# Gate and up sums of a SwiGLU feed-forward as Strassen block products on one Trainium2 core

## The chip, the cores and the metric

The program runs on one core of one Trainium2 chip. The metric is the device time of one execution in microseconds (us). A core has engines that run side by side, each with its own queue in a fixed order: TensorE (PE, matrix products; PEld is its weight load), VectorE (DVE), ScalarE (ACT), GpSimd (POOL) and SyncE (SP), which here issues most transfers. The transfers themselves run on 16 DMA engines. SBUF is the working memory of 128 partitions, PSUM the memory that takes the products.

## The reference

Two decoder layers over 512 tokens of 1024 features: layer 0 mixes with a causal Conformer convolution, layer 1 with differential attention. Each is followed by a SwiGLU feed-forward of 2816 hidden features and by a gated per-layer embedding. The change touches the first line of the feed-forward:

```python
def rms_norm(x, g):
    xf = x.astype(jnp.float32)
    y = xf * lax.rsqrt(jnp.mean(xf * xf, axis=-1, keepdims=True) + EPS)
    return (y * g.astype(jnp.float32)).astype(x.dtype)

def swiglu(x, w_gate, w_up, w_down):
    return (jax.nn.silu(x @ w_gate) * (x @ w_up)) @ w_down
...
    h = x
    for i in range(DEPTH):
        ...
        u = rms_norm(h, ffn_norm_g[i])
        h = h + swiglu(u, ffn_w_gate[i], ffn_w_up[i], ffn_w_down[i])
        gate = jax.nn.sigmoid(rms_norm(h, ple_norm_g[i]) @ ple_w_gate[i])
        h = h + gate * (p[i] @ ple_w_proj[i])
```

## The kernel before

Activations lie transposed: h[c] (L166) holds 128 features by 512 tokens, eight of them. Every product of two float32 matrices is made of three products of float32r parts: a value is split into a rounded part (hi) and the rest (lo), and mm3 (L153 to L157) adds lo x hi, hi x lo and hi x hi in PSUM. One mm3 over a block of 128 features is three matmuls, each with its own weight load.

A weight tile is 128 x 1024, 512 KB: 128 output features by 1024 inputs, in eight blocks of 128 (wpart, L159). weight() (L137) takes the next tile of the program's order: a transfer on SP's queue into wraw (two buffers), a cast on ACT into whi (L148), a subtraction on DVE, or for a few tiles on POOL, into wlo (L150). whi and wlo have four buffers each, so weights run up to four tiles ahead.

Norm (L172) holds the scaled activations norm.u as 8 pairs of hi and lo tiles (tags A0 to A15). The scale per token isn't applied there: squares are added on POOL (L189), columns() sums them with small products, POOL takes the power (L214), and rows() spreads the result over the partitions into rb, which is multiplied into the sums afterwards.

ffn() (L566) cuts the 22 hidden chunks of 128 into parts of 8, 8 and 6 (PARTS). For each chunk it takes a gate and an up tile, adds 8 blocks x 3 matmuls of 512 tokens for each into PSUM (tags mm with four banks, sc and tp with two each), multiplies both by rb (L582, L584, DVE), applies Silu (L583, ACT), multiplies (L585) and splits the result into hl (L587, L588, tag B). After a part linear() (L538) multiplies its hidden chunks by w_down, two outputs at a time for the first two, one at a time after, and adds them to h (L592). Then ple() (L598) makes the gated embedding; its factors pp wait since the stage before, those of chunks 6 and 7 of layer 0 in one of the two buffers of tag C4, those of layer 1 in one each of C2, C3 and C4 and in D2 and D3. The last chunk of layer 1's ple runs in two cuts of 256 tokens (CUTS, L52).

Tags name buffers: sb(shape, tag, bufs) gives one of bufs buffers and waits until one is free. The order of each engine's queue is not written out by hand; a list scheduler places the instructions by priority (the order of the program) and by its own times. wk (4 buffers) and big (5) are scratch tiles of 512 tokens.

Of the kernel before, what the change touches and what calls it, by code (L numbers as in the profile page):

```python
# [12 lines left out]
F32 = mybir.dt.float32  # L13
F32R = mybir.dt.float32r
# [6 lines left out]
P = 128  # L21
# [57 lines left out]
GLO = 1  # L79
QKV = (("q", 0, (0, 0, 0, 0)), ("v", 0, (0, 1, 1, 0)), ("q", 1, (1, 1, 2, 2)), ("q", 2, (0, 1, 2, 0)), ("v", 1, (1, 2, 2, 2)), ("q", 3, (0, 2, 0, 1)))  # L80
# [3 lines left out]
def trunk(ctx, tc, xT, pT, wts, diag, dww, vec, rel, onehot, lamv, out):  # L84
# [22 lines left out]
    f = lambda ap: ap.bitcast(F32)  # L107

# [240 lines left out]
    def phased_out(c):  # L349
# [5 lines left out]
        both_ = sb([P, 2, S], f"B{c}", 1)  # L355
# [12 lines left out]
    def other_taps(c):  # L368
# [13 lines left out]
        yc = sb([P, 2, S], f"B{c}", 1)  # L382
# [183 lines left out]
    def ffn(norm, after):  # L566
        rb = None
        for at, (f0, n) in enumerate(PARTS):
            hid = []
            for i in range(n):  # L570
                wg, wu = weight(), weight()
                pg, pu = mm(), mm()
                for k in range(NC):
                    mm3(pg, wpart(wg, k), norm.u[k], k == 0, k == NC - 1)
                if rb is None:
                    norm.diagonal()
                for k in range(NC):
                    mm3(pu, wpart(wu, k), norm.u[k], k == 0, k == NC - 1)
                if rb is None:
                    rb = norm.rows()  # L580
                tg, tu = big(), big()
                V.tensor_tensor(tg, pg, rb, ALU.mult)  # L582
                A.activation(tg, tg, AF.Silu)  # L583
                V.tensor_tensor(tu, pu, rb, ALU.mult)  # L584
                V.tensor_tensor(tu, tu, tg, ALU.mult)  # L585
                hl = sb([P, 2, S], f"B{i}", 1, F32R)
                A.copy(hl[:, 0], tu)  # L587
                V.tensor_tensor(hl[:, 1], tu, f(hl[:, 0]), ALU.subtract)  # L588
                hid.append((hl[:, 0], hl[:, 1]))

            def add(m, acc):
                V.tensor_tensor(h[m], acc, h[m], ALU.add)  # L592
                if at == len(PARTS) - 1:
                    after.chunk(m)

            linear(n, hid, add, 2)
# [30 lines left out]
    ffn(norm, n2)  # L627
# [65 lines left out]
    def values(s, ws, tb, between):  # L693
        acc, r = tokens(ws, tb, between)
        vt_ = sb([P, 4, 2, P], f"B{4 * s + tb}", 1, F32R)
# [217 lines left out]
    ffn(norm, n2)  # L913
# [132 lines left out]
```

## Time and profile before

| what | value |
|---|---|
| time, 3 runs | 1306.6, 1307.61, 1310.06 us (median 1307.61) |
| span of the profiled execution | 1308.0 us |
| 0 to 229 us, convolution | PE busy 216.8, DVE 166.1, POOL 101.1 us |
| 229 to 613 us, feed-forward and ple of layer 0 | PE 384.0 of 384, DVE 174.8, ACT 114.9, POOL 20.6 us |
| 613 to 905 us, attention | PE 279.2 of 292, DVE 218.4, POOL 111.8 us |
| 905 to 1274 us, feed-forward and ple of layer 1 | PE 369.0 of 369, DVE 163.1, ACT 108.1, POOL 14.6 us |

The profile is that of one execution, taken by the hardware profiler. A group or timeline row reads: line, engine, operation, output tile <- input tiles, output shape <- input shape, count, then the busy time and the mean duration of one in ns, then the idle time of the engine before it and what ended it. L numbers are lines of the kernel before. Consecutive instructions of one engine overlap at their ends, so what one costs its queue is read from the starts of a row of them. The windows view gives the busy time of each engine in a stretch of the span, the TensorE clock that was granted there (1.00 is full speed), the share of time that the 16 DMA engines were busy and the bytes moved per second.

### The profile page before, as it was taken

The numbers are of one execution on the slowest core, as the hardware profiler recorded it, in microseconds if no ns is written. First come the engines' busy times: TensorE is split into PE (matmuls) and PEld (weight loads), VectorE is DVE, ScalarE is ACT, GpSimd is POOL, SyncE is SP. The second block draws the span as 40 slices with busy tenths as digits, with TensorE's granted clock in tenths as the row PEclk, the third lists the DMA queues.
The fourth block names the chain that finished last, engine by engine and source line by source line (L and its number), as shares of the span: only waits on it lengthen the run. The fifth ranks groups of instructions, "written<-read, shape, count | busy, mean of one in ns | idle before, by whom it ended". The sixth has DMA issues, their size and how long they took to land. (4 is left out here: it accounts for less than half of the span.)

```text
span 1308.0 us, 15405 instructions
## 1 busy us (share of the span) xinstructions
PE 1278.6 (98%) x5904; PEld 1055.7 (81%) x5904; DVE 741.2 (57%) x1142; ACT 522.1 (40%) x827; POOL 248.2 (19%) x207
## 2 busy tenths in 40 slices
PE   8999999999999999999999998999999999999998
PEld 5888678888888888888888886878888888888887
DVE  6898646444344434456678888845543344334445
ACT  5642445332122212254566667734332233223332
POOL 4754323000000000032335535122000000000030
PEclk8999889999999999999999998999999999999999
DMA  6654313322323232232222211213323223222231
GB/s 219 229 166 156 106 33 129 96 98 87 106 96 97 88 104 94 80 122 83 80 91 92 89 58 59 87 48 114 97 97 97 97 97 97 97 97 89 83 119 65
DMA packets 46838, 131.97 MB, mean 101 GB/s; under 512 B 5379, under 2 KB 9987, under 8 KB 46764
## 3 DMA queue, kind: packets, MB, share of 16 engines
q1 hardware_dynamic: 44640, 127.55, 29.6%
q10 hardware_dynamic: 2124, 3.43, 0.8%
q8 instruction: 46, 0.75, 0.2%
q14 instruction: 28, 0.23, 0.1%
HBM read 126.75 MB, written 4.21 MB: 100 GB/s over the span
## 5 line engine op out<-in xcount | busy, mean ns | idle before, releaser
L148 ACT CAST whi<-wraw 128x1024 fp32r<-128x1024 f32 (+2 forms) x214 | 218.6, 1026 | 566.3 <-PE mm L157 349.5
L155 PE MATMUL mm<-A,wlo 128*128 128x512 f32 (+1 forms) x1096 | 423.9, 391 | 4.8 <-ACT A L169 2.7
L156 PE MATMUL mm<-A,whi 128*128 128x512 f32 (+1 forms) x1096 | 428.0, 392 | 0.4
L157 PE MATMUL mm<-A,whi 128*128 128x512 f32 (+1 forms) x1096 | 425.3, 389 | 0.0
L150 DVE TENSOR_TENSOR wlo<-wraw,whi 128x1024 fp32r<-128x1024 f32 (+2 forms) x210 | 260.5, 1244 | 70.9 <-ACT whi L148 70.6
L155 PEld LDWEIGHTS mm<-A,wlo 128*128 128x128 f32 x1096 | 206.2, 188 | 49.6 <-DVE wlo L150 3.7
L156 PEld LDWEIGHTS mm<-A,whi 128*128 128x128 f32 x1096 | 206.6, 188 | 46.4 <-DVE A L170 3.0
L157 PEld LDWEIGHTS mm<-A,whi 128*128 128x128 f32 x1096 | 206.6, 188 | 43.1 <-issue 1.0
L189 POOL TENSOR_TENSOR acc<-acc,wk 128x512 f32<-128x512 f32 x42 | 67.4, 1604 | 787.7 <-issue 660.2
L156 PE MATMUL mm<-B,whi 128*128 128x512 f32 x352 | 137.5, 391 | 0.0
L157 PE MATMUL mm<-B,whi 128*128 128x512 f32 x352 | 137.5, 391 | 0.0
L155 PE MATMUL mm<-B,wlo 128*128 128x512 f32 x352 | 137.2, 392 | 0.0
L592 DVE TENSOR_TENSOR h<-mm,h 128x512 f32<-128x512 f32 x48 | 33.0, 691 | 122.7 <-PE mm L157 122.7
L584 DVE TENSOR_TENSOR big<-mm,rb 128x512 f32<-128x512 f32 x44 | 30.4, 691 | 126.2 <-PE mm L157 126.2
L582 DVE TENSOR_TENSOR big<-mm,rb 128x512 f32<-128x512 f32 x44 | 30.4, 691 | 99.4 <-PE mm L157 93.0
L157 PEld LDWEIGHTS mm<-B,whi 128*128 128x128 f32 x352 | 66.1, 188 | 14.6
L155 PEld LDWEIGHTS mm<-B,wlo 128*128 128x128 f32 x352 | 66.1, 188 | 14.2
L156 PEld LDWEIGHTS mm<-B,whi 128*128 128x128 f32 x352 | 66.0, 188 | 14.2
L157 PE MATMUL mm<-whi,A 128*128 128x512 f32 x192 | 75.6, 395 | 0.0
L156 PE MATMUL mm<-wlo,A 128*128 128x512 f32 x192 | 75.0, 396 | 0.0
L155 PE MATMUL mm<-whi,A 128*128 128x512 f32 x192 | 74.8, 397 | 0.0
L214 POOL TENSOR_TENSOR r<-v,mhalf 128x8 f32<-128x8 f32 (+1 forms) x31 | 47.4, 1529 | 122.8 <-DVE v L212 100.4
(198 smaller groups left out, 1402.0 us busy)
## 6 DMA issues: line engine op xcount, KB each, us to landing
wraw<-in_wts SPq DMA_DIRECT2D x194, 512.0 KB, 3.5
wraw<-in_wts SPq DMA_DIRECT2D x16, 384.0 KB, 2.9
D<-in_diag SPq DMA_DIRECT2D x22, 256.0 KB, 4.9
C<-in_diag SPq DMA_DIRECT2D x16, 256.0 KB, 4.7
h<-in_xT SPq DMA_DIRECT2D x8, 256.0 KB, 5.6
bias<-scr ACTq DMA_DIRECT2D x8, 256.0 KB, 3.3
out_t<-h SPq DMA_DIRECT2D x7, 256.0 KB, 2.0
wraw<-in_wts SPq DMA_DIRECT2D x4, 256.0 KB, 5.2
```

Of the source, the lines that this page charges most:

```text
L148: A.copy(hi[:, cut], raw[:, cut])
L150: eng.tensor_tensor(lo[:, cut], raw[:, cut], f(hi[:, cut]), ALU.subtract)
L155: T.matmul(acc, al, bh, start=first, stop=False)
L156: T.matmul(acc, ah, bl, start=False, stop=False)
L157: return T.matmul(acc, ah, bh, start=False, stop=last)
L189: self.last = self.eng.tensor_tensor(self.acc, self.acc, sq, ALU.add)
L214: last_pow[0] = G.tensor_tensor(r[:, :n], v[:, :n], mhalf[:, :n], ALU.pow)
L582: V.tensor_tensor(tg, pg, rb, ALU.mult)
L584: V.tensor_tensor(tu, pu, rb, ALU.mult)
L592: V.tensor_tensor(h[m], acc, h[m], ALU.add)
```

## The change

The gate sum of two neighbouring chunks is a product of a 256 x 1024 weight block by 1024 x 512 activations. The change halves all three sides: the outputs (chunk c and chunk c+1), the inputs (blocks 0 to 3 and 4 to 7) and the tokens (0 to 255 and 256 to 511), and takes Strassen's seven products of half blocks in place of eight; the same for the up sum. It does so for 10 of the 11 pairs of chunks of each feed-forward. The first pair (PLAIN) keeps the old code.

- combinations(), once per feed-forward, scales h by the gain on ACT, makes the five sums and differences of activation blocks on POOL, each 128 x 1024, and splits each on ACT and DVE; the two other operands are halves of norm.u. They live in buffers of the tags in SPACE.
- operands() makes the weight sides of the seven products. Tile z takes the first half of one weight tile and the second half of the other, by SP; d, its difference, is made on POOL. Tile x is loaded by SP with the first halves of both tiles, and a transfer on POOL's queue adds the second halves to it in flight (accum_op). Tile y is loaded with the first weight tile, and a transfer adds the second. So there are three plain and two adding transfers of 512 KB where there were two plain ones. Each of z, x, y (128 x 1024) and d (128 x 512) is split on ACT and DVE.
- strassen() makes the products, each of 4 blocks x 3 matmuls of 256 tokens, and sums them to o1 and o2: one copy and two half copies on ACT, four operations on DVE.
- After the gate's two outputs, the gain rb is applied on DVE for one and on POOL for the other; the same for the up outputs; then product and split for both as before. Each of o1 and o2 holds half the tokens of one chunk and half of the other, which the strided writes of spot() sort out.
- B tiles are now allocated in pairs (btile), in the convolution and the attention too.

```diff
@@ -77,6 +77,13 @@
 PACK = True
 E1 = True
 GLO = 1
+H2 = S // 2
+SPACE = (
+    ((("C0", 2, 4), ("C1", 2, 4), ("C2", 2, 4), ("C3", 2, 4), ("wth", 2, 2), ("wtl", 2, 2)), ("C5", "C5"), "C4"),
+    ((("C0", 2, 4), ("C1", 2, 4), ("C5", 2, 4), ("D0", 1, 2), ("D1", 1, 2), ("D4", 1, 2), ("D5", 1, 2), ("wth", 2, 2), ("wtl", 2, 2)), ("C2", "C3"), "C4"),
+)
+PLAIN = ((0, 0),)
+DMASUM = True
 QKV = (("q", 0, (0, 0, 0, 0)), ("v", 0, (0, 1, 1, 0)), ("q", 1, (1, 1, 2, 2)), ("q", 2, (0, 1, 2, 0)), ("v", 1, (1, 2, 2, 2)), ("q", 3, (0, 2, 0, 1)))
...
@@ -105,6 +112,13 @@
     wk = lambda dt=F32, shape=(P, S): sb(list(shape), "wk", 4, dt)
     big = lambda dt=F32, shape=(P, S): sb(list(shape), "big", 5, dt)
     f = lambda ap: ap.bitcast(F32)
+    bpair = [None]
+    def btile(i, dt=F32):
+        if i % 2 == 0:
+            bpair[0] = sb([P, 2, 2, S], f"B{i // 2}", 1, dt)
+        return bpair[0][:, i % 2]
...
@@ -563,30 +577,167 @@
     linear(NC, z, add_conv, 3, first=(None, last_add[0], scaled[1]))
-    def ffn(norm, after):
+    def ffn(norm, after, space):
         rb = None
+        homes, xtags, ztag = space
+        slots = [(t, n, k) for t, n, k in homes for _ in range(n)]
+        def home():
+            t, n, k = slots.pop(0)
+            if k == 4:
+                w = sb([P, 4, H2], t, n, F32R)
+                return [w[:, 0:2], w[:, 2:4]]
+            two = [sb([P, 2, H2], t, n, F32R)]
+            t, n, k = slots.pop(0)
+            return two + [sb([P, 2, H2], t, n, F32R)]
+        def combinations():
+            us = [sb([P, 2, 2, S], f"B{1 + j}", 1) for j in range(2)]
+            us = [t.rearrange("p a b s -> p (a b) s") for t in us]
+            for c in range(NC):
+                A.activation(us[c // 4][:, c % 4], h[c], AF.Copy, scale=col(norm.g, c))
+            b = [[us[k][:, :, t * H2 : (t + 1) * H2] for t in range(2)] for k in range(2)]
+            sums = sb([P, 2, 2, S], "B3", 1).rearrange("p a b (u s) -> p a (b u) s", u=2)
+            made = {}
+            for i, (name, x, y, op) in enumerate((
+                (3, b[1][1], b[0][1], ALU.subtract), (4, b[0][0], b[1][0], ALU.subtract),
+                (1, b[0][0], b[1][1], ALU.add),
+                (6, b[0][0], b[0][1], ALU.add), (7, b[1][0], b[1][1], ALU.add),
+            )):
+                if not DMASUM and name in (3, 4):
+                    x, y = y, x
+                t = sums[:, i % 2]
+                G.tensor_tensor(t, x, y, op)
+                his, los = home(), home()
+                for k in range(2):
+                    A.copy(his[k], t[:, 2 * k : 2 * k + 2])
+                    V.tensor_tensor(los[k], t[:, 2 * k : 2 * k + 2], f(his[k]), ALU.subtract)
+                made[name] = [(his[k // 2][:, k % 2], los[k // 2][:, k % 2]) for k in range(4)]
+            made[2] = [tuple(t[:, :H2] for t in norm.u[k]) for k in range(4)]
+            made[5] = [tuple(t[:, H2:] for t in norm.u[4 + k]) for k in range(4)]
+            return made
+        def source(i, mstep, kh):
+            return bass.AP(wts.tensor, wts.offset + i * P * 1024 + kh * S, [[1024, P], [mstep, 2], [1, S]])
+        turn = [0]
+        def two_parts(raw, shape=(P, 1024)):
+            hi = sb([P, 1024], "whi", 4, F32R)
+            lo = sb([P, 1024], "wlo", 4, F32R)
+            n = raw.shape[-1]
+            A.copy(hi[:, :n], raw)
+            V.tensor_tensor(lo[:, :n], raw, f(hi[:, :n]), ALU.subtract)
+            return hi, lo
+        def operands(i):
+            m2 = 2 * P * 1024
+            turn[0] += 1
+            z = sb([P, 2, S], ztag, 2 if ztag[0] == "C" else 1)
+            nc.sync.dma_start(z, source(i, m2 + S, 0))
+            x = sb([P, 2, S], xtags[turn[0] % 2], 2)
+            nc.sync.dma_start(x, source(i, m2, 0))
+            y = sb([P, 1024], "wraw", 2)
+            nc.sync.dma_start(y, wts[i])
+            nc.gpsimd.dma_start(x, source(i, m2, 1), accum_op=ALU.add)
+            nc.gpsimd.dma_start(y, wts[i + 2], accum_op=ALU.add)
+            z = z.rearrange("p a s -> p (a s)")
+            d = big()
+            G.tensor_tensor(d, z[:, :S], z[:, S:], ALU.subtract)
+            zp = two_parts(z)
+            dp = two_parts(d)
+            xp = two_parts(x.rearrange("p a s -> p (a s)"))
+            yp = two_parts(y)
+            half = lambda w, j: tuple(t[:, j * S : (j + 1) * S] for t in w)
+            return {3: half(zp, 0), 4: half(zp, 1), 1: half(dp, 0), 5: half(xp, 0), 2: half(xp, 1), 6: half(yp, 0), 7: half(yp, 1)}
+        def swapped(t):
+            return bass.AP(t.tensor, t.offset + H2, [list(t.ap[0]), [-H2, 2], [1, H2]])
+        def halves(t):
+            return t.rearrange("p (a s) -> p a s", a=2)
+        def strassen(i, b):
+            w = operands(i)
+            def product(acc, name):
+                for k in range(4):
+                    mm3(acc, wpart(w[name], k), b[name][k], k == 0, k == 3)
+            vp, mp = mm(), tp()
+            product(vp[:, H2:], 3)
+            product(vp[:, :H2], 4)
+            product(mp[:, :H2], 1)
+            o1 = big()
+            o2 = wk()
+            A.copy(o2, vp)
+            A.copy(o1[:, :H2], mp[:, :H2])
+            A.mul(o1[:, H2:], mp[:, :H2], -1.0)
+            V.tensor_tensor(o1, vp, o1, ALU.add)
+            qp = mm()
+            product(qp[:, :H2], 5)
+            product(qp[:, H2:], 2)
+            V.tensor_tensor(halves(o2), swapped(qp), halves(o2), ALU.subtract)
+            V.tensor_tensor(o1, o1, qp, ALU.subtract)
+            xp = sc()
+            product(xp[:, H2:], 6)
+            product(xp[:, :H2], 7)
+            V.tensor_tensor(o1, xp, o1, ALU.add)
+            return o1, o2
+        comb = None
         for at, (f0, n) in enumerate(PARTS):
             hid = []
-            for i in range(n):
...
+            for pair in range(n // 2):
+                if (at, pair) in PLAIN:
+                    for i in range(2):
+                        wg, wu = weight(), weight()
...
+                        hl = btile(2 * pair + i, F32R)
+                        A.copy(hl[:, 0], tu)
+                        V.tensor_tensor(hl[:, 1], tu, f(hl[:, 0]), ALU.subtract)
+                        hid.append((hl[:, 0], hl[:, 1]))
+                    continue
+                if comb is None:
+                    comb = combinations()
+                i = wnext[0]
+                wnext[0] += 4
+                gs = strassen(i, comb)
+                for eng, t in zip((V, G), gs):
+                    eng.tensor_tensor(t, t, rb, ALU.mult)
+                    A.activation(t, t, AF.Silu)
+                us = strassen(i + 1, comb)
+                hl = sb([P, 2, 2, S], f"B{pair}", 1, F32R)
+                for eng, t, g, o in zip((V, G), us, gs, (0, 1)):
+                    eng.tensor_tensor(t, t, rb, ALU.mult)
+                    V.tensor_tensor(t, t, g, ALU.mult)
+                    def spot(k):
+                        a = hl.offset + k * S + (2 * S if o else 0)
+                        return bass.AP(hl.tensor, a, [list(hl.ap[0]), [H2 - 2 * S if o else H2 + 2 * S, 2], [1, H2]])
+                    A.copy(spot(0), halves(t))
+                    V.tensor_tensor(spot(1), halves(t), f(spot(0)), ALU.subtract)
+                for k in range(2):
+                    hid.append((hl[:, k, 0], hl[:, k, 1]))
             def add(m, acc):
...
@@ -624,7 +775,7 @@
                 gate(*part)
     n2 = Norm("ple_g0")
-    ffn(norm, n2)
+    ffn(norm, n2, SPACE[0])
     norm = Norm("attn_g")
...
@@ -692,7 +843,7 @@
     def values(s, ws, tb, between):
         acc, r = tokens(ws, tb, between)
-        vt_ = sb([P, 4, 2, P], f"B{4 * s + tb}", 1, F32R)
+        vt_ = btile(4 * s + tb, F32R).rearrange("p a (h d) -> p (a h d)", h=4).rearrange("p (h a d) -> p h a d", h=4, a=2)
...
@@ -910,7 +1061,7 @@
     linear(NC, ot, add_attn, 2, heads_until, step)
     n2 = Norm("ple_g1")
-    ffn(norm, n2)
+    ffn(norm, n2, SPACE[1])
```

More of the change, by code (lines that the diff above doesn't have):

```diff
@@ L354, in phased_out @@
         nc.scalar.dma_start(d, o)
-        both_ = sb([P, 2, S], f"B{c}", 1)
+        both_ = btile(c)
         for g in range(NPH):
@@ L381, in other_taps @@
                 G.tensor_tensor(pacc, pacc, pr, ALU.add)
-        yc = sb([P, 2, S], f"B{c}", 1)
+        yc = btile(c)
         if c == 0:
```

33 lines of the change are left out of this document (14 added, 19 removed).

## The prediction

> **What bounds the kernel now.** I read the page first: its span, the busy shares and the chain that ended last.
>
> ```profile
> span 1308.0 us, 15405 instructions
> PE 1278.6 (98%) x5904; PEld 1055.7 (81%) x5904; DVE 741.2 (57%) x1142; ACT 522.1 (40%) x827; POOL 248.2 (19%) x207
> ```
>
> TensorE (PE) is busy 98% of the span, so a shorter stream of products is the only large gain; the question is who becomes late. Next the busy times by stage. Columns: stretch, length, busy us of PE, weight load, DVE, ACT and POOL, then the granted clock, the DMA share and GB/s.
>
> ```profile
> 0.00:150.00 150.00, 141.23 (x727) 115.66 (x728) 120.10 (x140) 73.38 (x104) 78.85 (x67) 0.98 0.55 186
> 250.00:550.00 300.00, 300.00 (x1320) 247.61 (x1320) 127.13 (x148) 79.53 (x94) 0.00 (x0) 1.00 0.29 95
> 30.00:35.00 5.00, 5.00 (x24) 4.13 (x23) 4.66 (x8) 4.02 (x8) 1.67 (x2) 1.00 1.04 406
> ```
>
> The second row is the first feed-forward: PE without a gap at clock 1.00, DVE at 42%, Pool idle, the DMA engines at 0.29. So every product removed there counts in full, until another engine fills up. Third, the matmuls in order of time at the end, where the last chunk already runs in two cuts of 256 tokens:
>
> ```profile
> 1279.79 0.39 PE L157 MATMUL mm<-A,whi 128*128 128x512 f32 x1
> ...
> 1297.46 0.39 PE L157 MATMUL mm<-A,whi 128*128 128x512 f32 x1
> 1297.69 0.28 PE L155 MATMUL mm<-A,wlo 128*128 128x256 f32 x1
> ...
> 1303.32 0.28 PE L157 MATMUL mm<-A,whi 128*128 128x256 f32 x1
> ```
>
> The starts give the price; the durations (0.39, 0.28) overlap. 78 steps of 512 columns: 17.67 / 78 = 0.2265 us. 47 steps of 256: 5.63 / 47 = 0.1198 us, 6 ns more than half. That is the first loss of the change.
>
> **The products.** Chunks 0 and 1 stay plain; 10 pairs of chunks for gate and for up, in two layers, are 40 Strassen sums. Each was 2 chunks x 8 blocks x 3 = 48 wide matmuls: 48 x 0.2265 = 10.87 us. Now 7 x 4 x 3 = 84 narrow ones: 84 x 0.1198 = 10.06 us. Gain 0.81 us each, **32.5 us** in all: 7.5% and not Strassen's 12.5%, since each narrow matmul pays its 6 ns. A pair (gate and up) goes from 21.75 to 20.12 us, and that is what every other engine now has to meet.
>
> **DVE in a pair.** Its forms and their means, first without Pool (250 to 600 us), then beside it (0 to 150 us), and one stretch in order of time:
>
> ```profile
> L150 DVE TENSOR_TENSOR wlo<-wraw,whi 128x1024 fp32r<-128x1024 f32 x58 | 70.7, 1223 | 15.4 <-ACT whi L148 15.4
> L584 DVE TENSOR_TENSOR big<-mm,rb 128x512 f32<-128x512 f32 x20 | 13.8, 692 | 62.8 <-PE mm L157 62.8
> L170 DVE SCALAR_TENSOR_TENSOR A<-h,vec,A 128x512 fp32r<-128x512 f32 x8 | 5.9, 746 | 0.0
> ```
>
> ```profile
> L393 DVE SCALAR_TENSOR_TENSOR sc<-C,C,sc 128x512 f32<-128x512 f32 x69 | 51.9, 752 | 1.5
> L150 DVE TENSOR_TENSOR wlo<-wraw,whi 128x1024 fp32r<-128x1024 f32 x17 | 24.8, 1459 | 8.0 <-ACT whi L148 7.9
> L170 DVE SCALAR_TENSOR_TENSOR A<-h,vec,A 128x512 fp32r<-128x512 f32 x8 | 11.8, 1519 | 0.5 <-ACT A L169 0.4
> ```
>
> ```profile
> 240.54 0.68 DVE L584 TENSOR_TENSOR big<-mm,rb 128x512 f32<-128x512 f32 x1
> 241.13 0.68 DVE L582 TENSOR_TENSOR big<-mm,rb 128x512 f32<-128x512 f32 x1
> 241.73 1.22 DVE L150 TENSOR_TENSOR wlo<-wraw,whi 128x1024 fp32r<-128x1024 f32 x1
> 242.87 0.69 DVE L585 TENSOR_TENSOR big<-big,big 128x512 f32<-128x512 f32 x1
> ```
>
> Back to back, a 512-wide operation takes 0.60 us of the queue and a 1024-wide one 1.14. A Strassen sum has three weight splits of 1024 and one of 512 (3 x 1.14 + 0.60 = 4.02) and four output sums with an operand in PSUM (2.40). Per pair that is 12.84, plus six operations behind it (two gains, two products, two splits; 3.60): **16.4 us**, where before it was 4 x 1.14 + 8 x 0.60 = 9.4.
>
> On top comes Pool. In the first 150 us, with Pool busy 53%, the split went from 1223 to 1459 ns and L170 from 746 to 1519, while L393, with one operand in PSUM, stayed at 752. How one meeting looks:
>
> ```profile
> 608.67 1.48 DVE L150 TENSOR_TENSOR wlo<-wraw,whi 128x1024 fp32r<-128x1024 f32 x1 [0.44 <-ACT whi L148]
> ...
> 609.31 1.99 POOL L189 TENSOR_TENSOR acc<-acc,wk 128x512 f32<-128x512 f32 x1 [0.24 <-ACT wk L188]
> ...
> 610.08 1.77 DVE L612 TENSOR_TENSOR big<-big,D 128x512 f32<-128x512 f32 x1
> ```
>
> Here one Pool sum cost DVE 0.26 + 1.08 = 1.3 us. The change puts four such Pool operations in each pair (two differences of weights, two gains). Fourteen of DVE's 22 operations have both inputs in SBUF. Lower end: 14 x 0.24 us x (share of Pool 0.32 / 0.53) = 2 us per pair; upper: 4 x 1.3 = 5.2. I take 3.0, nearer the mean of many than the single meeting. DVE then needs 19.4 of 20.12 us, 97%. (The Trainium skill, SBUF — State Buffer, "Who interferes with whom", states this: a DVE operation with two SBUF inputs and a GpSimd one that reads SBUF block each other, and one SBUF input doesn't contend. The trace agrees with the 752 beside the 1519, and the rule speaks against moving work to Pool.)
>
> Buffers give slack of several us: weight parts turn through four slots, PSUM holds two Strassen sums. So 97% need not stall PE, but queues in fixed order leave bubbles. Nothing shows them; between 0 and 1.6 us per pair (at which the gain is gone) I take 0.4: **+8 us**.
>
> **ACT and Pool.**
>
> ```profile
> L148 ACT CAST whi<-wraw 128x1024 fp32r<-128x1024 f32 x194 | 202.9, 1051 | 518.0 <-PE mm L157 322.2 <-issue 158.2 <-DMA wraw<-in_wts 27.6
> L587 ACT CAST B<-big 128x512 fp32r<-128x512 f32 x44 | 27.4, 623 | 19.6 <-DVE big L585 19.5
> L189 POOL TENSOR_TENSOR acc<-acc,wk 128x512 f32<-128x512 f32 x42 | 67.4, 1604 | 787.7 <-issue 660.2 <-ACT wk L188 126.9
> L150 POOL TENSOR_TENSOR wlo<-wraw,whi 128x1024 fp32r<-128x1024 f32 x4 | 9.6, 2397 | 9.1 <-issue 9.1
> L214 POOL TENSOR_TENSOR r<-v,mhalf 128x8 f32<-128x8 f32 x16 | 28.5, 1778 | 32.6 <-ACT wth L797 13.9 <-DVE v L212 11.9 <-DVE st L786 4.8
> 30.34 0.33 SPq L145 DMA_DIRECT2D wraw<-in_wts  x1
> ```
>
> ACT per pair, even at full durations: 6 casts x 1.05, about 8 operations of 0.62 and four halves (under 0.62 each): under 14 us, covered. Pool: 4 x 1.6 = 6.4 us, and four issues of adding transfers. No Pool issue is in the trace: from 0.33 us (SP's) to 1.78 (Pool's slowest small operation) I take 1.0; 10.4 us, covered. But each adding transfer waits in Pool's queue for its base to land, and the weight difference and the gain of the second output stand behind it. The difference feeds product 1 and the gain only the hidden parts, both several us later, so I cost that at nothing while bases land early; a base that lands late would cost its whole delay beyond that.
>
> Once per layer Pool makes five sums of activations, 5 x 2.4 = 12 us, under the plain pair (21.75 us); their casts and splits add 10 x 0.6 us to DVE's 9.4. That hides, except that one sum may stand ahead of the norm's power on Pool: 0 to 2.4 us, I take 1.2 per layer: **+2.4**.
>
> At the end of a part the last output needs one sum, gain, product, cast and split, 5 x 0.6 = 3 us; linear() runs 6 chunks x 2 x 3 x 0.2265 = 8.2 us first (n = 8), 5.4 (n = 6). Covered unless DVE is behind: 0 to 2 us, 0.5 at each of six: **+3**.
>
> **Transfers.**
>
> ```profile
> wraw<-in_wts SPq DMA_DIRECT2D x194, 512.0 KB, 3.5
> ```
>
> At 95 GB/s the share is 0.29, so one 512 KB tile takes 0.524 MB / 95 x 0.29 = 1.60 us of all 16 engines; at 406 GB/s it is 1.34. A Strassen sum has three plain loads and two adding ones where two plain ones were. If adding costs as one transfer, 5 x 1.34 to 1.60 = 6.7 to 8.0 of 10.06 us: covered. If it costs as two, 7 x 1.34 = 9.4 or 7 x 1.60 = 11.2. Nothing in the trace adds in flight. I take two at 1.34, the row of the fuller queue: 93%, covered with nothing to spare. (The Trainium skill, Collectives: The Full Stack, "The bandwidth ceiling: the fold count and why AG ≠ RS ≠ AR", says that an add in the DMA engine needs two source reads and so runs at half rate; no run here shows it yet.) The chain load, issue, add, cast, split (3.5 + 1 + 3.5 to 7 + 2.2) is 10 to 14 us, and x and y have two buffers, 20 us. z has one free buffer (its tag's other slot holds a ple product): load, cast and split take 6 us of 10.06. SP's queue carries all three loads, so a z that waits holds x and y behind it.
>
> **Sum.** -32.5 + 8 + 2.4 + 3 = -19.1; 1308.0 - 19.1 = 1288.9 us. The profiled span is 0.4 above the median of the runs, 1307.6, so I forecast **1288.5**.
>
> **Rivals.**
> 1. Nothing is late: 1307.6 - 32.5 = 1275. For it: slots and PSUM hold two sums. Against: 97% and 93% on two engines.
> 2. DVE becomes the bound. It decides once Pool costs it more than 3.7 us per pair, and beyond 5.3 (21.75 - 16.4) the kernel is slower than before. If each Pool operation stops DVE for its whole 1.6 us: 22.8 us per pair, 20 x 1.05 = +21, with the other 5.4: 1334. For it: the 1519. Against: the 1459, and outputs read from PSUM.
> 3. The DMA engines become the bound, **slower**: adding costs two transfers at 1.60, 11.2 us per sum against 10.87, +13, with 5.4: 1326. Slower as soon as an adding transfer takes over (10.87 - 3 x 1.60) / 2 = 3.0 us of the engines; at 4.8 (three transfers) 14.4 us per sum, +141: 1449. For it: twice the bytes and an operation never measured here. Against: 406 GB/s.
> 4. The narrow matmul doesn't hold 0.1198, since its weight load shows 0.19 us: 84 x 0.188 = 15.8, +197. Against: 48 in a row did.
>
> **Chances.** Forecast, 1277 to 1303: 0.50. Rival 1, 0.08. DVE, 1302 to 1334: 0.18. DMA, 1305 and up: 0.20. Others, slower: 0.04. Within 0.3% (4 us), about what a measurement of this kernel tells from no change, falls a third of rival 2 and the edge of 3: 0.08. Faster 0.62, slower 0.30. The range runs from rival 1 to where most of 2 and half of 3 lie: 1275 to 1326.
>
> **What would show it.** Matmul steps of 0.12 us in the gate and up stage, 20.1 to 20.6 us per pair; DVE at 90% or more there, its two-SBUF operations longer than 1223 and 692 ns and those from PSUM not; DMA share 0.75 to 0.95. Wrong if PE's waits name wlo after DMA (rival 3) or after Pool and DVE (rival 2), or if the clock falls below 1.00.

## The result and the profile after

The changed kernel takes 1369.37 us (median of 4 runs, 1367.01 to 1372.14) against 1307.77 for the kernel before in the same session: ratio 1.0469, 95% interval 1.0451 to 1.0487. It is slower by 61.6 us; the forecast was 19 us faster, and the range ended at 1326. The page of after, its busy shares, two of its DMA queues and its transfers:

```profile
span 1365.1 us, 19474 instructions
PE 1265.1 (93%) x7344; PEld 1102.4 (81%) x7344; DVE 962.4 (71%) x1362; ACT 643.7 (47%) x1063; POOL 464.3 (34%) x377
q1 hardware_dynamic: 60640, 148.52, 33.8%
q0 software_dynamic: 16640, 41.95, 18.2%
wraw<-in_wts SPq DMA_DIRECT2D x154, 512.0 KB, 3.9
C<-in_wts SPq DMA_DIRECT2D x80, 512.0 KB, 5.5
C<-in_wts POOLq DMA_DIRECT2D x40, 512.0 KB, 6.3
wraw<-in_wts POOLq DMA_DIRECT2D x40, 512.0 KB, 7.8
```

PE does 13.5 us less work (1278.6 before) and stands still for 100 us of the span, where before it stood still for 29. No engine is full: DVE has 71%, both queues together 52% of the DMA engines. So the place has to be found by stage. The lengths between the last sums into h of each stage, in us:

| stage | before | after | e6 | k2 |
|---|---|---|---|---|
| convolution | 222.9 | 225.1 | 220.9 | 229.3 |
| feed-forward 0 | 360.7 | 390.0 | 358.2 | 355.2 |
| ple 0 and attention | 313.6 | 313.6 | 312.3 | 311.0 |
| feed-forward 1 | 360.8 | 387.9 | 354.7 | 354.3 |

Nearly all of it is in the two feed-forwards, +29.3 and +27.1 of 57.1 us of the span (e6 and k2 are runs below). A stretch with nothing but Strassen sums, by the windows view (stretch, length, busy PE, weight load, DVE, ACT, POOL, then clock, DMA share, GB/s), and PE's waits for split weights over the whole run (total, times, longest):

```profile
385.00:425.00 40.00, 34.03 (x274) 32.87 (x272) 29.34 (x34) 17.34 (x27) 13.80 (x13) 1.00 0.81 198
```

```profile
PE mm L169 <- DVE wlo L633: 35.4, 33, 1.5
PE tp L169 <- DVE wlo L633: 14.9, 19, 1.9
PE sc L169 <- DVE wlo L633: 2.1, 2, 1.8
```

The clock is 1.00 and PE waits for split weights, 54 times and for 52.4 us in all, while DVE itself has time (73% here) and the DMA engines too (0.81). Something that isn't an engine's work is late. One turn of the order of time (start, duration, engine, line) shows what:

```profile
402.98 2.01 DVE L633 TENSOR_TENSOR wlo<-C,whi 128x1024 fp32r<-128x1024 f32 x1
405.02 0.37 SPq L643 DMA_DIRECT2D C<-in_wts  x1
...
411.32 1.23 POOL L646 DMA_DIRECT2D C<-in_wts  x1 [7.41 <-DVE big L681]
...
412.11 1.77 POOL L650 TENSOR_TENSOR big<-C 128x512 f32<-128x512 f32 x1
...
413.90 0.37 SPq L641 DMA_DIRECT2D C<-in_wts  x1
413.91 0.62 ACT L632 CAST whi<-big 128x512 fp32r<-128x512 f32 x1 [4.22 <-POOL big L650]
...
414.43 1.04 ACT L632 CAST whi<-C 128x1024 fp32r<-128x1024 f32 x1
...
416.36 2.01 DVE L633 TENSOR_TENSOR wlo<-C,whi 128x1024 fp32r<-128x1024 f32 x1
...
424.61 1.23 POOL L646 DMA_DIRECT2D C<-in_wts  x1 [7.32 <-DMA C<-in_wts]
```

The split of x ends at 404.99 and frees its buffer; SP loads the base of the x after next (L643; the base is the plain load that the adding transfer is added to); Pool issues the adding transfer (L646) 6.3 us later. Behind L646 in Pool's queue stands d (L650), which belongs to the sum before. ACT casts d and then x, since its queue has them in that order, and the next split of x starts at 416.36 and ends at 418.37: 13.4 us after the last. SP's load of z (L641) leaves when d is done, too. So five queues (DVE, SP, the DMA engines, Pool, ACT) make a **ring**: split x, free its buffer, load the base, issue, d, cast, split. It turns once in a sum, and 13.4 us stand in place of 10.06. For L646 at 411.32 the profile names a DVE sum as what it waited for; one turn later, 13.3 us on, it names the base, and over all 40 issues that wait is the largest (92.0 of 267.7 us).

### The profile page after: what moved, and what is told of

Its sections match the earlier page's. It is cut to its first block, busy times and chain, and to the rows that moved or that the text cites. A ratio compares the mean times of both kernels' runs of the same rounds, so it can differ in the third digit from the quotient of the medians.

```text
span 1365.1 us, 19474 instructions
## 1 busy us (share of the span) xinstructions
PE 1265.1 (93%) x7344; PEld 1102.4 (81%) x7344; DVE 962.4 (71%) x1362; ACT 643.7 (47%) x1063; POOL 464.3 (34%) x377
## 3 DMA queue, kind: packets, MB, share of 16 engines
q0 software_dynamic: 16640, 41.95, 18.2%
## 5 line engine op out<-in xcount | busy, mean ns | idle before, releaser
L169 PE MATMUL mm<-A,wlo 128*128 128x512 f32 (+1 forms) x776 | 266.2, 350 | 30.8 <-DVE wlo L633 27.1
L170 PE MATMUL mm<-A,whi 128*128 128x512 f32 (+1 forms) x776 | 268.4, 347 | 2.9 <-DVE A L184 1.4
L171 PE MATMUL mm<-A,whi 128*128 128x512 f32 (+1 forms) x776 | 266.6, 344 | 0.0
L164 DVE TENSOR_TENSOR wlo<-wraw,whi 128x1024 fp32r<-128x1024 f32 (+2 forms) x130 | 166.2, 1285 | 77.1 <-ACT whi L162 76.9
L162 ACT CAST whi<-wraw 128x1024 fp32r<-128x1024 f32 (+2 forms) x134 | 134.4, 1010 | 172.3 <-DMA wraw<-in_wts 99.7
L169 PEld LDWEIGHTS mm<-A,wlo 128*128 128x128 f32 x776 | 147.2, 190 | 54.5 <-issue 29.4
L170 PEld LDWEIGHTS mm<-A,whi 128*128 128x128 f32 x776 | 147.4, 190 | 24.0 <-DVE A L184 4.7
L171 PEld LDWEIGHTS mm<-A,whi 128*128 128x128 f32 x776 | 147.3, 190 | 17.5 <-issue 0.5
L633 DVE TENSOR_TENSOR wlo<-C,whi 128x1024 fp32r<-128x1024 f32 x80 | 120.2, 1503 | 44.5 <-ACT whi L632 44.5
L646 POOL DMA_DIRECT2D C<-in_wts x40 | 49.6, 1241 | 267.7 <-DMA C<-in_wts 92.0
L632 ACT CAST whi<-C 128x1024 fp32r<-128x1024 f32 x80 | 83.8, 1047 | 81.7 <-PE mm L171 47.3
L169 PE MATMUL mm<-C,wlo 128*128 128x256 f32 (+1 forms) x336 | 101.0, 301 | 14.3 <-DVE wlo L633 8.3
L170 PE MATMUL mm<-C,whi 128*128 128x256 f32 (+1 forms) x336 | 98.7, 294 | 0.0
L171 PE MATMUL mm<-C,whi 128*128 128x256 f32 (+1 forms) x336 | 98.7, 294 | 0.0
```

The costliest lines, as they stand in the source:

```text
L162: A.copy(hi[:, cut], raw[:, cut])
L164: eng.tensor_tensor(lo[:, cut], raw[:, cut], f(hi[:, cut]), ALU.subtract)
L169: T.matmul(acc, al, bh, start=first, stop=False)
L170: T.matmul(acc, ah, bl, start=False, stop=False)
L171: return T.matmul(acc, ah, bh, start=False, stop=last)
L632: A.copy(hi[:, :n], raw)
```

## The experiments

Theory **Q** (queues): the ring, not a full engine, sets after's time. Rivals: **D**, the DMA engines are the bound since adding costs two transfers or more; **V**, Pool's work beside DVE's is the bound.

**e1_d_first**: the adding transfers stand behind the d of the sum before.

```diff
-            nc.gpsimd.dma_start(x, source(i, m2, 1), accum_op=ALU.add)
-            nc.gpsimd.dma_start(y, wts[i + 2], accum_op=ALU.add)
+            with tc.issue_after(last_d[0].ins) if last_d[0] else nullcontext():
+                nc.gpsimd.dma_start(x, source(i, m2, 1), accum_op=ALU.add)
+                nc.gpsimd.dma_start(y, wts[i + 2], accum_op=ALU.add)
...
-            G.tensor_tensor(d, z[:, :S], z[:, S:], ALU.subtract)
+            last_d[0] = G.tensor_tensor(d, z[:, :S], z[:, S:], ALU.subtract)
```

> The adding transfers of x and y are held back in POOL's queue until the weight difference d of the sum before has been issued; all work stays. Theory Q (a ring through queues in fixed order: x's split frees its buffer, the load of x lands 6.3 us later, the adding transfer waits for it in POOL's queue, d waits behind it, the casts and x's split behind d; 13.4 us per sum): the ring is open, the period falls to the next bound, 11 us if that is the DMA engines (1310 to 1325 us), 10.1 if PE (about 1290). Theory D (the DMA engines' capacity alone sets 13.4): 1365 to 1370, no change. Theory V (DVE slowed by POOL): no change, 1360 or more.

**e2_d_on_dve**: d is made by DVE (`V.tensor_tensor(d, ...)`), so that no computation that PE waits for stands behind a transfer on Pool.

> The weight difference d moves from POOL to DVE; POOL's queue keeps the waits of the adding transfers, and nothing of the weights stands behind them. Q: a second cut through the same ring, so about what the reordering gave, 1328 to 1345 (DVE gets 1.2 us more per pair and loses the meetings with d). If the ring is not the cause: 1365 or more.

**e3_no_adds**: the two adding transfers are left out (x and y hold only their bases).

> Leaves the two adding transfers of each Strassen sum out, so the tiles x and y hold only the first addend and the output differs; three plain loads and all other work stay. Q: nothing in POOL's queue waits for a load, period near 10.1 us, 1285 to 1300. D: the engines carry 4.8 us per sum, 1285 to 1300. V: DVE and POOL's four operations per pair are as before, 1340 or more.

**e4_plain_for_add**: plain transfers in the same place (without `accum_op`; x and y hold the second half only). **e6_first_and_plain**: the same in e1's order.

> The two adding transfers become plain ones of the same bytes on the same queue, with the same waits; they overwrite x and y, so the output differs. Q: the ring stays and only the landings shorten; 1330 to 1369. D: five transfers at 1.6 us are 8 us per sum, under PE's 10.1, 1285 to 1300. V: 1360 or more. The share of the software queue also tells the engine time of an adding transfer beside a plain one of the same size (1.6 expected for plain, 3.1 read for adding).

> The reordering of e1_d_first, and plain transfers in place of the adding ones (they overwrite x and y, so the output differs). D: what is left of e1_d_first over e3_no_adds (43 us) is the engine time of adding, 3.1 us each, 11 us per sum; with 5 x 1.57 = 7.9 us the time falls to 1292 to 1300. If the waits in POOL's and SP's queues set the rest, it stays near e4_plain_for_add, 1310 to 1320.

**e5_weights_once**: the operands are made once in a part and used for all its sums, so the Strassen sums load, split and add nearly no weights.

> Loads, sums and splits the weight operands once for each part and uses them for all its Strassen sums, so the output differs; products, output sums, gains and hidden splits stay. All theories: the price of the products themselves. 84 steps of 0.12 us against 48 of 0.2265 give 1275 to 1282 (1307.6 less 32.5, plus ends of parts); if it stays over 1300 the narrow products or the sums of the outputs cost more than forecast, and neither ring nor transfers are the whole cause.

Times: e1 1335.45 (ratio 1.0199, 1.0145 to 1.0252), e2 1318.77, e3 1292.22, e4 1316.63, e5 1291.68, e6 1296.56 us (two executions of e1, one each of the others). e3 and e6 lie where Q and D put them; e1 is above Q's 1325, e2 below its 1328, e4 between D's 1300 and Q's 1330, e5 above its 1282. The same stretch of the windows view, one fence for each of e1, e2, e3 and e6:

```profile
385.00:425.00 40.00, 37.22 (x298) 37.04 (x297) 33.33 (x40) 19.41 (x31) 15.67 (x14) 0.96 0.88 215
```

```profile
385.00:425.00 40.00, 38.07 (x314) 37.52 (x313) 34.02 (x44) 20.52 (x32) 11.57 (x10) 1.00 0.94 241
```

```profile
385.00:425.00 40.00, 40.00 (x336) 40.00 (x335) 37.78 (x44) 23.11 (x37) 12.79 (x8) 1.00 0.51 158
```

```profile
385.00:425.00 40.00, 40.00 (x336) 40.00 (x335) 35.41 (x43) 21.90 (x34) 16.92 (x15) 1.00 0.77 252
```

Order alone (e1) gives back 33.9 us with the same work, and e2, which opens the ring in another way, 50.6: Q holds for after. Then the DMA engines are fuller (0.88 in e1, 0.94 in e2), and PE still stands still for 7 and 5% of the stretch. e6 has e1's order with plain transfers in place of the adding ones: 38.9 us less, and PE without a gap. So adding itself holds the kernel once the ring is open, as D says. Not all that e1 has left is the DMA engines, though: e2 makes the same transfers, is 16.7 us faster, and its engines are fuller. And a plain transfer takes less of the engines and also lands sooner (5.3 and 5.0 us for x and y in e6, 7.9 and 7.9 in e1); e6 doesn't separate the two. V falls: in e3 DVE is busy 37.78 of 40 us and PE doesn't wait.

e4 takes the adding out and keeps the old order: 52.7 us less than after, and e6 is 20.1 below e4. So the ring and the price of adding are not independent, and what each is worth depends on which goes first.

The price of adding is in q0. In e4 the same 41.95 MB cross it plain:

```profile
q0 software_dynamic: 11520, 41.95, 9.5%
```

9.5% of e4's span of 1314.5 us for 80 transfers is 1.56 us of all 16 engines for each; in after 18.2% of 1365.1 us is **3.11**. Adding costs twice a plain transfer, with 1.44 times the packets. (The Trainium skill, Collectives: The Full Stack, "The bandwidth ceiling: the fold count and why AG ≠ RS ≠ AR", says of ReduceScatter that its add in the DMA engine reads two sources and so gives half the rate; the trace agrees, 3.11 against 1.56.) A sum takes 3 x 1.56 + 2 x 3.11 = 10.9 us of the engines, and PE needs 10.06. The stretches above give somewhat less: a sum moves 2.62 MB, and by DMA share and GB/s that is 10.7 us of the engines in after and e1 and 10.2 in e2, still more than PE needs.

**e7_power_first** and **e8_alternate** take e1 on: the sums of activations go behind the norm's power on Pool, and e8 leaves five pairs of chunks plain in place of one (24 sums), so that the DMA engines can catch up.

```diff
-                G.tensor_tensor(t, x, y, op)
+                with tc.issue_after(last_pow[0].ins):
+                    G.tensor_tensor(t, x, y, op)
...
-PLAIN = ((0, 0),)
+PLAIN = ((0, 0), (0, 2), (1, 1), (1, 3), (2, 1))
```

> e1_d_first, and in each feed-forward POOL makes the five activation sums only after the norm's power. All work stays. If the sums ahead of the power cause the late rb, the wait for PSUM and the clock dip at the start (8 us per layer in e5_weights_once), 5 to 16 us less than e1_d_first: 1320 to 1331. If DVE's ten splits beside POOL's sums are the cause, no change, 1333 to 1340.

> e7_power_first with 6 of 11 pairs of chunks as Strassen sums and 5 plain ones between them (24 sums per two layers and matrix pair in place of 40). All work stays. If the DMA engines are what is left (11 us per Strassen sum, 3.1 us per plain one, so 28 of 42 us per two pairs), the transfers hide, and 24 x 0.81 = 19.5 us less, plus 4 to 12 us for starts and ends of stretches: 1292 to 1300. If each change between plain and Strassen costs a stall of several us, 1305 to 1320.

e7 1341.34 us (1.0249, 1.0215 to 1.0282), e8 1315.72 (1.0055, 1.0035 to 1.0074): both miss what they were built for; e8 lies in its second range, 1305 to 1320, but no row here shows that range's cause. The timelines of PE and POOL in e7, and its window:

```profile
260.63 0.55 PE L169 MATMUL tp<-C,wlo 128*128 128x256 f32 x1 [8.63 <-DVE wlo L635]
...
263.98 0.38 PE L169 MATMUL mm<-A,wlo 128*128 128x256 f32 x1
```

```profile
251.40 2.66 POOL L613 TENSOR_TENSOR B<-B 128x1024 f32<-128x1024 f32 x1 [1.30 <-DVE C L617]
254.02 1.71 POOL L653 TENSOR_TENSOR big<-C 128x512 f32<-128x512 f32 x1
```

```profile
250.00:275.00 25.00, 16.37 (x124) 16.19 (x123) 22.50 (x23) 12.82 (x21) 15.38 (x10) 0.80 0.70 168
```

The power came early, but the first d now stands behind all five sums, and PE waits 8.63 us for it. Behind that wait sixteen narrow matmuls take 3.56 us (their starts, 260.63 to 264.19), where 0.12 each would be 1.9, and the granted clock over these 25 us is 0.80.

**e10_two_plain**: e2 (d on DVE), two plain pairs at the start, and the activation sums made in the second of them, behind the power.

> e2_d_on_dve with two plain pairs at the start of each feed-forward in place of one, the five activation sums made beside the second and after the norm's power. All work stays. If the crowding of POOL and DVE at the start costs some 8 us per layer, it goes, and 4 Strassen sums fewer give back 3.2: 1318.8 less 8 to 13, 1305 to 1311. If the start costs nothing more than the one plain pair hides, 1320 to 1324.

1309.03 us, ratio 1.0009 (0.9993 to 1.0025): level with before, in the expected range. The crowding at the start went in part only: measured against what their sums should save, the two first parts still lose 9.9 and 7.8 us (12.7 and 13.8 in e2). In the same stretch as above:

```profile
385.00:425.00 40.00, 38.59 (x320) 38.22 (x320) 35.66 (x46) 21.99 (x35) 10.31 (x9) 1.00 0.98 249
```

The next three take adding transfers away by making the sums on the chip. **f1_sums_on_pool**: tile x is loaded plain with the two half blocks that z leaves, and d, x and y are all made on Pool; **f2_sums_on_pool_d_dve**: the same with d on DVE; **f3_one_sum_on_pool**: e10 with x alone made so.

```diff
-            nc.gpsimd.dma_start(x, source(i, m2, 1), accum_op=ALU.add)
-            nc.gpsimd.dma_start(y, wts[i + 2], accum_op=ALU.add)
...
+            G.tensor_tensor(y, z, bass.AP(x.tensor, x.offset + S, [list(x.ap[0]), [-S, 2], [1, S]]), ALU.add)
+            G.tensor_tensor(x, x, z, ALU.add)
```

> The start of e10_two_plain; no adding transfer: z and a tile x with the two other half blocks are loaded plain (two transfers per sum, as before the change), and POOL makes d, y and x from them (1.7, 2.4 and 2.4 us). All work stays. D: the DMA engines are free again (3.1 us per sum); POOL carries 16 of 20 us per pair, and if its meetings with DVE cost as in e3_no_adds, PE leads: 36 sums x 0.81 = 29 us less, with starts and ends 1280 to 1290. V: if DVE loses 0.7 us to each us of POOL, 22 us per pair or more: 1315 to 1340.

> f1_sums_on_pool with d on DVE: POOL 12.8 of 20 us per pair, DVE 1.2 us more. D: 1280 to 1290, below f1 if POOL is what holds f1, above it if DVE is. V: 1310 to 1330.

> e10_two_plain (36 sums, weight difference on DVE), but x is loaded plain as the other two blocks and z is added to it by one Pool operation of 1024 columns; y is still made by an adding transfer. Theory D: transfers fall from 10.9 to 4 plain plus 1 adding less one plain, 3 x 1.56 + 3.11 = 7.8 us per sum, share about 0.75, and the 36 sums keep most of their 29.2 us: 1282 to 1292. Rival V (Pool's work beside DVE's, which f1 and f2 showed as the bound once Pool does three such operations per sum): two operations of some 3.5 us in each pair lengthen DVE's two-SBUF operations; DVE then needs 17.6 + 3 to 5 us of 20.12 per pair, and PE waits for wlo and for d: 1300 to 1325, DVE at 95% or more in the second part.

f1 1358.68 us (1.0384, 1.0369 to 1.0400), f2 1369.27 (1.0466, 1.0450 to 1.0482), f3 1334.19 (1.0197, 1.0173 to 1.0222). All three are slower than both forecasts; V, which had the direction right, was 9 us short for f3 and 19 and 39 for f1 and f2. f1's stretch, and its DVE groups from 250 to 600 us:

```profile
385.00:425.00 40.00, 32.85 (x265) 31.72 (x263) 39.58 (x35) 17.29 (x28) 26.67 (x12) 1.00 0.26 86
```

```profile
L634 DVE TENSOR_TENSOR wlo<-C,whi 128x1024 fp32r<-128x1024 f32 x36 | 47.0, 1324 | 1.7 <-ACT whi L633 1.7
L634 DVE TENSOR_TENSOR wlo<-wraw,whi 128x1024 fp32r<-128x1024 f32 x18 | 41.6, 2309 | 7.6 <-ACT whi L633 7.6
L634 DVE TENSOR_TENSOR wlo<-big,whi 128x512 fp32r<-128x512 f32 x18 | 25.1, 1397 | 0.1
...
L686 DVE TENSOR_TENSOR wk<-mm,wk 128x512 f32<-128x512 f32 x18 | 12.3, 681 | 2.3 <-PE mm L171 2.3
```

The DMA engines are at 0.26, and DVE is full: its operations with two SBUF inputs take longer beside Pool, the splits of z and d about twice as long (2309 ns against 1223 before; 1397 against some 690), those of x and y 1324, while those with one in PSUM stay at 681. (That is the rule of the Trainium skill's SBUF — State Buffer, "Who interferes with whom", once more; here it decides the time, in after it wasn't the bound.) So what Pool may take over is small.

What was left of e10 could be the DMA engines or a fixed price at the start. **g1_five_plain** and **g2_four_plain** are e10 with more plain pairs: 24 and 28 sums. The edit of g2:

```diff
-PLAIN = ((0, 0), (0, 1))
+PLAIN = ((0, 0), (0, 1), (1, 2), (2, 1))
```

> e10_two_plain with three more pairs of chunks left plain (the second and fourth pair of the second part, the second of the third): 24 Strassen sums in place of 36. Theory D (what is left in e10_two_plain is the DMA engines, at 10.9 us of their time per sum against 10.06 of products): the plain pairs, with 6.2 us of transfers in 21.75, let the engines catch up, so the 24 sums keep their 0.81 us each, 19.4 us, less 3 to 6 for the starts and ends: 1292 to 1296, DMA share below 0.8 over each stretch of 40 us behind the first part, no stall of PE there. Rival (each feed-forward pays a fixed price of some 14 us at its start and between its parts, whatever the DMA engines do): every sum that is taken out loses its 0.81, 12 x 0.81 = 9.7 us more than e10_two_plain, about 1319.

> e10_two_plain with two more pairs left plain (the third of the second part, the second of the third): 28 sums. Theory D: 28 x 0.81 = 22.7 less 3 to 8, 1289 to 1295 where the engines catch up, up to 1300 where two Strassen pairs in a row (four sums, 43.6 us of transfers in 40.2) outrun the two buffers. Rival of a fixed price: 8 x 0.81 = 6.5 more than e10_two_plain, about 1315.5.

g1 1307.24 us (0.9984, 0.9967 to 1.0001), g2 1305.13 (0.9964, 0.9947 to 0.9981): between the two theories, as if both held in part. Behind the first part of layer 0, g2 is 7.9 us shorter than before (254.9 against 262.8), where 10 sums x 0.81 = 8.1; e10, with 14 sums there, only 4.6. The first part is 4.7 us longer (102.6 against 97.9), though its 4 sums should save 3.2. DVE's and PE's timelines of g2 there:

```profile
238.25 2.89 DVE L233 TENSOR_TENSOR wk<-ident,r 128x512 f32<-128x512 f32 x1
241.07 3.42 DVE L164 TENSOR_TENSOR wlo<-wraw,whi 128x1024 fp32r<-128x1024 f32 x1
244.41 4.69 DVE L617 TENSOR_TENSOR C<-B,C 128x512 fp32r<-128x512 f32 x4
249.02 1.21 DVE L164 TENSOR_TENSOR wlo<-wraw,whi 128x1024 fp32r<-128x1024 f32 x1
250.16 0.68 DVE L713 TENSOR_TENSOR big<-mm,rb 128x512 f32<-128x512 f32 x1
```

```profile
250.89 0.50 PE L169 MATMUL mm<-A,wlo 128*128 128x512 f32 x1 [1.33 <-DVE big L713]
```

Beside Pool's sums of activations the norm's diagonal (L233) takes 2.89 us and a split 3.42, four splits of these sums follow, and the first gain, which frees PE's banks, is late. PE's wait for it is 1.33 us, a small part of the 7.9 us that the first part loses; these rows don't name the rest.

**h1_start_moved** and **h3_one_plain_behind** leave the whole first part plain and name the second chunk's gain as what the activation sums are to follow.

```diff
-                with tc.issue_after(last_pow[0].ins):
+                with tc.issue_after(gained[0].ins):
```

> The whole first part plain, and the third pair of the second part and the second of the third: 20 Strassen sums, as the start of each feed-forward has no Strassen sum that waits for the sums of activations, and Pool makes these behind the gain of the second chunk in place of behind the norm's power. In g2_four_plain the second and third part of each layer were 7.9 and 8.6 us shorter than before, 10 sums x 0.81 = 8.1, and the first part 4.7 us longer though it has 4 sums: 7.9 us lost at the start. Theory S (these 7.9 us come from Pool's sums and their splits beside the norm, and from the plain weights' splits that they delay): 20 x 0.81 = 16.2 us less than before and 0 to 4 lost, 1292 to 1297. Rival (the sums cost their time wherever they stand, by Pool's and DVE's meetings): some 8 us per layer stay lost, 1306 to 1309.

> h1_start_moved with one pair less left plain (the second of the third part): 24 sums, the last part all Strassen, six sums in a row. Theory D with S: 24 x 0.81 = 19.4 less up to 1.5 per layer where six sums in a row (65 us of transfers in 60 of products) outrun the buffers, less 0 to 4 at the start: 1289 to 1296. Rival: 1303 to 1306.

h1 1313.32 us (1.0039, 1.0021 to 1.0057), h3 1309.27 (1.0002, 0.9986 to 1.0018): both slower than either forecast. The edit did not do what it was to do: the gain is on DVE, Pool's queue got no order from it, and the sums ran ahead of the power. h1's timelines of POOL and PE:

```profile
231.04 5.18 POOL L613 TENSOR_TENSOR B<-B,B 128x1024 f32<-128x1024 f32 x2
237.52 2.71 POOL L613 TENSOR_TENSOR B<-B,B 128x1024 f32<-128x1024 f32 x1 [1.29 <-DVE C L617]
240.18 1.47 POOL L228 TENSOR_TENSOR r<-v,mhalf 128x4 f32<-128x4 f32 x1
```

```profile
253.45 0.50 PE L169 MATMUL mm<-A,wlo 128*128 128x512 f32 x1 [3.28 <-DVE big L714]
```

It shows one thing all the same: with no Strassen sum in it, the first part still takes 104.8 us against 97.9. So no Strassen sum is needed for the loss; what the first part has besides before is the activation sums, and PE waits 3.3 us for the gain behind them.

**k1_behind_rb** and **k2_behind_rb_five** put a small operation into Pool's queue that reads the norm's row rb, and the sums behind it; k1 is g2 otherwise, k2 leaves a fifth pair plain (24 sums). The edit of k2 against g2:

```diff
+            late = sb([P, P // 2], "v8", 2)[:, :8]
+            gate = G.tensor_tensor(late, rb[:, :8], rb[:, :8], ALU.add)
...
-                with tc.issue_after(last_pow[0].ins):
+                with tc.issue_after(gate.ins):
                     G.tensor_tensor(t, x, y, op)
...
-PLAIN = ((0, 0), (0, 1), (1, 2), (2, 1))
+PLAIN = ((0, 0), (0, 1), (0, 2), (1, 2), (2, 1))
```

> g2_four_plain (28 sums) with a small Pool operation that reads the norm's row rb ahead of the sums of activations, so that these run behind it: the norm's diagonal and the weight splits then run on DVE without Pool beside them, and the first gains stand ahead of the sums' splits. (In h1_start_moved the order did not come out as named: Pool's sums ran ahead of the norm's power, which stood at 240.18 in place of 236.80.) Theory S (the 8 us per layer lost in the first part are the sums that stand beside the norm): PE has no wait on the gain at some 250 us, the first part falls by 3 to 8 us per layer against g2_four_plain, 1290 to 1299. Rival (the sums cost their time wherever they stand, or the loss lies in the two Strassen pairs of the first part): 1303 to 1308.

> k1_behind_rb with the third pair of the first part plain too: 24 sums, one Strassen pair in the first part. If the rest of the loss lies in the four sums of the first part that follow each other (DMA engines at 0.94 in g2_four_plain at 290 to 310 us), this is level with k1_behind_rb or up to 4 us faster though it has 4 sums less, 1290 to 1297; if the sums lose nothing there, it is 4 x 0.81 = 3.2 us slower than k1_behind_rb.

k1 1302.07 us (0.9949, 0.9930 to 0.9968); k2 **1298.69 us, ratio 0.9913 (0.9886 to 0.9941)**: 0.9% faster than before. k1 lies between its theories, and its two first parts are 0.8 and 1.9 us shorter than g2's, where theory S asked for 3 to 8. Between g2 and k1, the order alone, the ratios' intervals overlap; between g1 and k2, both with 24 sums, they don't, but there the plain pairs differ too. In k2 the diagonal is back at 0.68 us, the gain comes right behind the row, and the waits view names one wait of PE in feed-forward 0 and none in feed-forward 1. The timeline of DVE and that view:

```profile
241.03 0.68 DVE L233 TENSOR_TENSOR wk<-ident,r 128x512 f32<-128x512 f32 x1
...
248.28 0.68 DVE L715 TENSOR_TENSOR big<-mm,rb 128x512 f32<-128x512 f32 x1
```

```profile
PE mm L169 <- DVE wlo L164: 0.3, 1, 0.3
```

k2 was a little faster than k1 with four sums less, as expected if the four sums of the first part that follow each other lose more than they gain.

## Why the prediction was wrong

The miss of 80.9 us (1369.4 - 1288.5) falls into three pieces by the runs: order on Pool's queue 33.9 (after to e1), the price of adding 38.9 (e1 to e6), all else 8.1 (e6 to the forecast). The first two together are 72.8 us; singly they depend on the path, since adding taken out first is worth 52.7 (after to e4) and the order behind it 20.1 (e4 to e6).

- **Products, -32.5: right.** 336 narrow matmuls in 40.00 us (e6) are 0.119 us each, forecast 0.1198. In e5 the 14 sums behind the first part of layer 0 save 12.6 us (250.2 against 262.8; 14 x 0.81 = 11.3). The clock stayed at 1.00 between stalls; rival 4 is out.
- **Pool's queue, at nothing: the step that failed first.** The prediction saw that an adding transfer waits in Pool's queue with d behind it, and let it go, "both several us later" and "while bases land early". But a base can't be loaded before the split of x two sums earlier frees its buffer, and that split stands behind d and its cast. The delay closes on itself, and the slack named (two buffers, 20 us) was counted once along a chain that comes back to its start.
- **Transfers, 9.4 of 10.06 us, "covered with nothing to spare": the size was wrong, and it decided.** The factor of two was right; the unit, 1.34 us from the fullest 5 us of before, was not: it is 1.56, so 10.9 us by the queues' shares and 10.2 to 10.7 by the stretches. The upper unit of the prediction's own range, 1.60, was the nearer one. Rival 3 set its point at 3.0 us for an adding transfer, and it measured 3.11. That its time, 1326, lies between e1 (1335) and e2 (1319) is luck: in e2 the parts behind the first are 3.7 and 2.3 us shorter than before, and what makes it slower is the two first parts, 7.8 and 8.9 us longer.
- **DVE, +8 for bubbles: the load was right, the bubbles were not there.** 97% was forecast, 89% (e6) and 94% (e3) measured with PE full. Rival 2 (1334) wasn't the bound of after; it is what f1, f2 and f3 ran into.
- **Start, +2.4: far too small.** In e5, with nearly no weights in the way, the first part of layer 0 takes 101.8 us where 97.9 - 6 x 0.81 = 93.0 was due: 8.8 us lost (8.6 in layer 1), forecast 1.2. PE stands still for 3.0 of them, 0.8 for the norm's diagonal and 2.1 for the first gain, and the clock is 0.85 from 245 to 255 us; the rest isn't taken apart. The sum ahead of the power was seen; that Pool's five sums stretch DVE's work on the norm, and that their splits stand ahead of the first gain, was not.
- **Ends of parts, +3:** not separated; g2's 7.9 of 8.1 leaves some 0.2 us behind the first part of layer 0.
- **Not forecast:** the convolution grew by 2.2 us in after and 6.4 in k2, where its arithmetic is unchanged. PE's wait for the tile D there went from 3.0 (before) to 6.4 us (after) and 6.5 (k2). In e6 the convolution is 2.0 us shorter than before, and 5.6 shorter than in e1, so that much of the 38.9 us lies there. The scheduler plans the queues anew with each edit; no run took this apart.

What stays open: k2's two feed-forwards save 12.0 us of the 19.4 that its 24 sums are worth, and its convolution gives 6.4 back. PE doesn't wait for the missing 7.4: it stands still for 0.3 and 0.1 us in the two. Of the 7.4, 6.4 lie in the two first parts, 99.6 and 99.5 us where 96.3 and 96.4 were due. But the table's borders are DVE's sums, and PE can run products on either side of them: what follows the two feed-forwards is 3.8 us shorter than before (2.6 in ple and attention, 1.2 at the end). So part of the 7.4, and of the losses in first parts above, may be products that changed sides; how much isn't shown.

The prediction's sign, PE's waits naming wlo after DMA (rival 3) or after Pool and DVE (rival 2), could not tell the two apart, nor show the ring: in after all 54 waits for split weights name DVE, which writes wlo, and the cause stands several steps behind. The order of Pool's queue, followed from a buffer's release round to its next release, could have shown the ring without a run.

## What to carry to other kernels

When a step puts a transfer that waits for another transfer into the queue of an engine that also computes, follow the buffer from one release to the next through every queue it passes; if the path returns to its start, the work can't turn faster than the path allows. Here the path took 13.4 us a sum, and two buffers of x didn't hide it; more were not tried. Price an add in flight at two plain transfers at the unit measured in the stage itself, and leave the DMA engines a margin: with the ring open PE stood still for 3.5% of the stretch at a share of 0.98 (e10), 4.8% at 0.94 (e2), and not at all at 0.77 (e6). Try once-per-layer preparation behind the first work that frees the products' banks: k2 has it there and gains, though how much of the gain is its place isn't shown.

## What the hardware showed

- 512 KB added in flight takes 3.11 us of all 16 DMA engines, 1.56 plain on the same queue; landing took 6.3 and 7.8 us (medians of x and y) against 4.7 and 5.6 plain in e4.
- On Pool an adding issue takes 1.24 us for x and 1.05 for y; a plain one of the same size on Pool takes 0.77 and 0.56 (e4), on SP 0.33 to 0.37:

```profile
L646 POOL DMA_DIRECT2D C<-in_wts x40 | 49.6, 1241 | 267.7 <-DMA C<-in_wts 92.0
L647 POOL DMA_DIRECT2D wraw<-in_wts x40 | 41.9, 1048 | 155.8 <-DVE wlo L164 72.2
```

- In the stretch shown DVE was busy 94% with PE never waiting (e3); at 99% (f1) and above (f3, 39.95 of 40 us) PE waited.
- Around one wait of PE of 8.63 us the granted clock of 25 us was 0.80, and the sixteen narrow matmuls behind it took 1.6 us more than usual (e7), so this stall cost more than its length.
